# Unused columns in the first SBUF pools, so that matmul operands start at multiples of 256 bytes

## The chip, the cores and the metric

One core of a Trainium2 chip runs the whole kernel. The metric is the device time of one execution in microseconds (us). The median of three runs of the kernel before is 2657.34 us (2654.69 to 2658.03). SBUF is the on-chip memory with 128 partitions; every tile takes the same byte range in each partition, and its start in that range is what the change moves. PSUM holds the sums that TensorE (PE) writes. VectorE (DVE), ScalarE (ACT), GpSimd (POOL) and the sync engine (SP) work beside it.

## The reference

The kernel computes a trunk of two layers on 1024 frames of width 1024. Layer 0 mixes frames by banded softmax attention, layer 1 by a gated delta rule; each is followed by a dense squared-ReLU MLP of width 4096:

```
for i in range(DEPTH):
    if i % N_MIXERS == 0:
        x = x + chunked_rel_attention(rmsnorm(x, ...), w_qkv, rel_bias, w_o)
    else:
        x = x + gated_deltanet(rmsnorm(x, ...), w_in, conv_w, ..., w_o)
    x = x + squared_relu_mlp(rmsnorm(x, mlp_norm[i]), mlp_w_up[i], mlp_w_down[i])
return rmsnorm(x, final_norm)

def squared_relu_mlp(h, w_up, w_down):
    return jnp.square(jax.nn.relu(h @ w_up)) @ w_down
```

## The kernel before, in words

Each dense product is made of three matmuls on rounded halves: an operand x is split into `hi` (x rounded to the type fp32r) and `lo` (x - hi), and hi·hi, hi·lo and lo·hi are summed in one PSUM bank (`products`, L267, for q, k, v and the projections; `block_product`, L994, for the MLPs). A matmul streams its moving operand (`xhi`, `xlo`: 512 columns of 4 bytes, 2048 bytes in each partition) past a stationary operand of 128 columns (`whi`, `wlo`, `ahi`, `alo`, `a`: 512 bytes).

The MLPs multiply 2x2 blocks in the seven-product form of Strassen and Winograd. One of the 16 units of the up stage (`up`, L1073) is seven calls of `block_product` with four k steps, so 12 matmuls each, in this order: s1·t1, s2·t2, 12·21, s3·t3, s4·22, 22·t4, and 11·11 of the next unit. The blocks 11, 12, s4 and 22 of the weights lie in `whi` and `wlo`; the sums s1, s2 and s3 lie in `ahi` and `alo`. One of the 32 units of the down stage (`down`, L1309) is seven blocks of six matmuls in nearly the same order; after each block DVE adds the bank to the residual (L1365). In the down stage the right-hand operands lie in pool hp for the even steps of b and, but for "11", in pool hx for the odd ones (`rows_part`, L1226).

Tiles come from pools that are stacked in SBUF in the order in which they are opened. `Trunk.__init__` (L207) opens const, wp, hp, sm and np, which stay. Each stage then opens its own: pp and pb in attention; xa, xb and hx in an MLP; dq, d1 and db in the DeltaNet layer. A tile's start follows from the sizes of all that lies below it. The order of the instructions of each engine is recorded by the Python code (a planner with a modelled clock in attention and DeltaNet, a written order in the MLPs); no size of a tile enters it.

Of the kernel before, what the change touches and what calls it, by code (L numbers as in the profile page):

```python
# [7 lines left out]
F32 = mybir.dt.float32  # L8
# [8 lines left out]
P = 128  # L17
# [3 lines left out]
HB = 512  # L21
# [22 lines left out]
class Paced:  # L44


    def __init__(self, gens, slots):
        self.gens, self.slots = list(gens), slots
        self.total, self.done, self.at, self.n = sum(n for _, n in gens), 0, 0, len(gens)
# [156 lines left out]
class Trunk:  # L206
    def __init__(self, ctx, tc, a, phases=5):  # L207
        self.tc, self.nc, self.a = tc, tc.nc, a
        nc = self.nc
        self.const = ctx.enter_context(tc.tile_pool(name="const", bufs=1))  # L210
        self.wp = ctx.enter_context(tc.tile_pool(name="wp", bufs=2))
        self.hp = ctx.enter_context(tc.tile_pool(name="hp", bufs=1))
        self.sm = ctx.enter_context(tc.tile_pool(name="sm", bufs=2))
        self.dr = ctx.enter_context(tc.tile_pool(name="dr", bufs=1, space=DRAM))
        self.np = ctx.enter_context(tc.tile_pool(name="np", bufs=1))
        self.acc = ctx.enter_context(tc.tile_pool(name="acc", bufs=2, space=PSUM))
        self.n = 0
        self.wq = nc.sync
        self.ident = self.const.tile([P, P], F32, name="ident")
        make_identity(nc, self.ident)  # L220
        self.ones = self.const.tile([P, 1], F32, name="ones")
        nc.vector.memset(self.ones, 1.0)
        self.norms = self.const.tile([P, 5, KT], F32, name="norms")
        nc.scalar.dma_start(self.norms, a["norms"])

    def nm(self, s):
        self.n += 1
        return f"{s}_{self.n}"
# [1276 lines left out]
    def deltanet(self, rhs, finish):  # L1505

        tc = self.tc
        with ExitStack() as es:
            self.tpp = es.enter_context(tc.tile_pool(name="tp", bufs=2, space=PSUM))
            self.sc = es.enter_context(tc.tile_pool(name="sc", bufs=2, space=PSUM))  # L1510

            self.dq = es.enter_context(tc.tile_pool(name="dq", bufs=1))
            self.d1 = es.enter_context(tc.tile_pool(name="d1", bufs=1))
            self.db = es.enter_context(tc.tile_pool(name="db", bufs=2))
            self.drhs, self.finish = rhs, finish
            self.aux = lambda: self.tpp.tile([P, HB], F32, name=self.nm("tp"), tag="tp")
            rings = {
                "tp": Ring(2, self.aux), "acc": Ring(2, self.bank), "nt": Ring(3, self.nt),
                "s1": Ring(2, lambda: self.sc.tile([P, P], F32, name=self.nm("s1"), tag="s1")),
                "s2": Ring(2, lambda: self.sc.tile([P, P], F32, name=self.nm("s2"), tag="s2"))}  # L1520
            for t, n in (("xp", 2), ("cy", 2), ("cz", 2)):
                rings[t] = Ring(n, lambda t=t, n=n: self.db.tile([P, 4 + HB], F32, name=self.nm(t), tag=t, bufs=n))
            self.begin(rings)
            self.silu_at, self.ready_at, self.solved = 0.0, set(), {}
            return self.timed(self.dn_run)
# [180 lines left out]
    def dn_gates(self):  # L1706
        nc, a, rhs = self.nc, self.a, self.drhs
        d1, db = self.d1, self.db
# [8 lines left out]
        self.kd = self.dr.tile([8, P, S], F32, name="kd")  # L1717
        self.ud = self.dr.tile([2, P, 32, 32], F32, name="ud")
        self.u12 = self.dr.tile([8, 2, 32, 8, 32], F32, name="u12")
        self.Zh = []  # L1720
        for n in range(2):
            z = d1.tile([P, 8, P], F32, name=f"Zh{n}")
# [22 lines left out]
        av, bv = t64("av"), t64("bv")  # L1745
        nc.sync.dma_start(av, abd[0:8].rearrange("h (p t) -> (h p) t", t=P))
        nc.sync.dma_start(bv, abd[8:16].rearrange("h (p t) -> (h p) t", t=P))
        nea = d1.tile([NQ, 1], F32, name="nea")
        mask = d1.tile([P, P], F32, name="mask")
        nc.gpsimd.memset(mask, 0.0)  # L1750
# [746 lines left out]
```

## Time and profile before

| | us |
|---|---|
| median of three runs | 2657.34 |
| the profiled execution's own time | 2660.0 |
| its span, first to last instruction | 2657.9 |
| PE busy | 2514.9 (95%) |
| DVE busy | 1890.5 (71%) |
| POOL busy | 1305.2 (49%) |
| ACT busy | 1225.5 (46%) |

The span falls into six stages: attention (to about 555 us), the first MLP (up to about 905, down to about 1217), DeltaNet (to about 1876), a short projection, and the second MLP (up from about 1985, down from about 2310). Matmuls are pipelined, and the end of one is modelled in the trace, so that durations overlap; what one costs in a stream is read from the distance between starts.

### The profile page before, as it was taken

The page shows a single profiled execution, that of the slowest core. Times are in us where ns is not written, and L with a number is a line of the kernel's source. Part 1 is how long each engine was busy: PE and PEld are TensorE (multiplying, and loading weights), DVE is VectorE, ACT ScalarE, POOL GpSimd, SP SyncE. Part 2 cuts the span into 40 slices and gives each one's busy share as a digit, 9 for nine tenths or more (in the row PEclk, how much of TensorE's full clock was granted, in tenths as well). Part 3 has the DMA queues.
Part 4 walks back from the last instruction along what each step waited for, and adds up shares of the span by engine and source line. Part 5 has one row for each costly group of instructions (what it writes and reads, how often), then busy time and mean ns, then how long its engine had stood idle before and what let it go on. Part 6 is the DMA issues. An engine that isn't in the chain of part 4 may idle for free.

```text
span 2657.9 us, 36117 instructions
## 1 busy us (share of the span) xinstructions
PE 2514.9 (95%) x12638; PEld 2062.5 (78%) x12638; DVE 1890.5 (71%) x3287; ACT 1225.5 (46%) x2269; POOL 1305.2 (49%) x1100
## 2 busy tenths in 40 slices
PE   8999999989999999998888999999989999999997
PEld 6888888868888777776677788888777888777775
DVE  6665656675454899987579977666675445799997
ACT  6665667444344444434663343433343434444443
POOL 2443456242322688886464333333042232688886
PEclk9999999999999999999998999999999999999998
DMA  4222225224233423323453122213323323432322
GB/s 158 66 70 71 67 83 167 99 87 144 102 114 108 151 99 104 107 88 107 117 142 102 53 75 66 72 62 115 108 87 136 118 97 117 152 102 96 107 91 80
DMA packets 141814, 271.78 MB, mean 102 GB/s; under 512 B 49264, under 2 KB 55856, under 8 KB 141632
## 3 DMA queue, kind: packets, MB, share of 16 engines
q1 hardware_dynamic: 120752, 227.51, 27.3%
q10 hardware_dynamic: 20880, 41.97, 4.2%
q8 instruction: 99, 1.62, 0.3%
q14 instruction: 83, 0.68, 0.1%
HBM read 193.24 MB, written 67.80 MB: 98 GB/s over the span
## 4 chain that ended last, share of the span: by engine, by line
PE 73%; DVE 15%; issue 5%; DMA 2%; ACT 2%; POOL 2%; SPq 0%; DVEq 0%; ACTq 0%; POOLq 0%
PE y L1000 22%; PE acc L161 17%; PE z L1000 10%; PE acc L1000 6%; PE tp L161 3%; PE s L161 3%; PE po L161 2%; PE pt L161 2%; PE sp L161 2%; DVE x L1365 2%; PE acc L272 2%; PE acc L271 2%; PE acc L273 2%; DVE a L1006 2%; DVE ft L161 1%
## 5 line engine op out<-in xcount | busy, mean ns | idle before, releaser
L161 PE MATMUL acc<-xhi,whi 128*128 128x512 f32 (+1 forms) x904 | 372.5, 412 | 9.4 <-DVE xp L161 9.4
L1015 POOL TENSOR_TENSOR s<-wraw 128x256 f32<-128x256 f32 (+1 forms) x93 | 101.0, 1086 | 556.0 <-DMA wraw<-in_w_up_dram 396.6
L161 PE MATMUL acc<-xlo,whi 128*128 128x512 f32 (+1 forms) x904 | 372.0, 412 | 0.7 <-DVE xlo L387 0.7
L161 PE MATMUL acc<-xhi,wlo 128*128 128x512 f32 x896 | 367.4, 410 | 3.4 <-POOL wlo L161 3.4
L161 POOL TENSOR_TENSOR wlo<-wraw,whi 128x512 fp32r<-128x512 f32 x126 | 167.9, 1333 | 244.8 <-ACT whi L161 196.5
L1009 ACT ACTIVATE xhi<-r 128x512 fp32r<-128x512 f32 x224 | 135.9, 628 | 256.5 <-POOL r L1012 207.2
L1006 DVE TENSOR_TENSOR wlo<-wraw,whi 128x512 fp32r<-128x512 f32 (+1 forms) x184 | 200.8, 1092 | 50.7 <-ACT whi L1009 47.4
L1000 PE MATMUL y<-xhi,whi 128*128 128x512 f32 x504 | 202.2, 401 | 14.8 <-DVE ssum L1083 8.7
L1000 PE MATMUL y<-xhi,wlo 128*128 128x512 f32 x504 | 201.8, 400 | 13.6 <-DVE wlo L1006 13.6
L1012 POOL TENSOR_TENSOR r<-r,r 128x512 f32<-128x512 f32 x124 | 202.9, 1638 | 14.8 <-DVE xlo L1006 10.2
L1000 PE MATMUL y<-xhi,a 128*128 128x512 f32 x488 | 180.2, 410 | 23.6 <-DVE x L1365 23.0
L1000 PE MATMUL y<-xlo,whi 128*128 128x512 f32 x504 | 200.7, 398 | 0.0
L161 PEld LDWEIGHTS acc<-xhi,whi 128*128 128x128 f32 (+1 forms) x904 | 171.9, 190 | 34.2 <-DVE xp L161 6.9
L161 PEld LDWEIGHTS acc<-xhi,wlo 128*128 128x128 f32 x896 | 171.0, 191 | 28.9 <-POOL wlo L161 4.7
L161 PEld LDWEIGHTS acc<-xlo,whi 128*128 128x128 f32 (+1 forms) x904 | 172.1, 190 | 24.9 <-DVE xlo L387 1.2
L1365 DVE TENSOR_TENSOR x<-y,x 128x512 f32<-128x512 f32 x240 | 163.8, 683 | 13.7 <-PE y L1000 11.8
L1009 ACT ACTIVATE whi<-wraw 128x512 fp32r<-128x512 f32 (+2 forms) x191 | 143.7, 766 | 37.5 <-ACT g L1086 12.7
L1083 DVE TENSOR_TENSOR ssum<-acc,nt 128x512 f32<-128x512 f32 x32 | 22.1, 691 | 189.1 <-PE acc L1000 189.1
L161 POOL TENSOR_SCALAR pr<-pr,rs 128x640 f32<-128x640 f32 (+4 forms) x128 | 88.6, 696 | 129.5 <-DVE rs L161 96.8
L1000 PEld LDWEIGHTS y<-xhi,a 128*128 128x128 f32 x488 | 92.6, 190 | 66.9 <-DVE x L1365 45.0
L161 POOL TENSOR_TENSOR cy<-cy,cz 128x512 f32<-128x512 f32 x48 | 69.1, 1439 | 145.6 <-DVE cz L161 131.5
L1004 POOL TENSOR_TENSOR xlo<-r,xhi 128x512 fp32r<-128x512 f32 x84 | 109.1, 1299 | 41.6 <-ACT xhi L1009 40.9
(349 smaller groups left out, 7131.1 us busy)
## 6 DMA issues: line engine op xcount, KB each, us to landing
wraw<-in_w_up_dram SPq DMA_DIRECT2D x64, 512.0 KB, 3.4
wraw<-in_w_down_dram SPq DMA_DIRECT2D x64, 512.0 KB, 3.9
r<-gd SPq DMA_DIRECT2D x112, 256.0 KB, 2.7
gd<-ssum ACTq DMA_DIRECT2D x64, 256.0 KB, 2.0
gd<-g ACTq DMA_DIRECT2D x64, 256.0 KB, 2.3
wraw<-in_w_in_dram SPq DMA_DIRECT2D x32, 512.0 KB, 3.5
wraw<-in_w_qkv_dram SPq DMA_DIRECT2D x30, 512.0 KB, 3.4
x<-xd SPq DMA_DIRECT2D x24, 512.0 KB, 5.0
```

What stands on the lines that cost most here:

```text
L161: return call(*args, **more)
L271: nc.tensor.matmul(ps, hi[:, k], xh, start=(k == 0), stop=False)
L272: nc.tensor.matmul(ps, hi[:, k], xl, start=False, stop=False)
L273: nc.tensor.matmul(ps, lo[:, k], xh, start=False, stop=(k == KT - 1))
L1000: nc.tensor.matmul(ps, w[:, k], x, start=bool(first and f), stop=bool(last and e), skip_group_check=True)
L1004: self.nc.gpsimd.tensor_tensor(lo, src, hi.bitcast(F32), ALU.subtract)
L1006: self.nc.vector.tensor_tensor(lo, src, hi.bitcast(F32), ALU.subtract)
L1009: self.nc.scalar.activation(hi, src, AF.Copy)
L1012: self.nc.gpsimd.tensor_tensor(out, x, y, ALU.subtract)
L1015: self.nc.gpsimd.tensor_tensor(out, x, y, ALU.add)
L1083: nc.vector.tensor_tensor(g, c, t, ALU.add)
L1365: nc.vector.tensor_tensor(x, ps, x, ALU.add)
```

## The change: what it does

Five tiles that nothing reads or writes are put into pools, and the three ring tiles of the convolution grow from 4 + 512 to 64 + 512 columns. Of these tiles the same columns are used as before.

```diff
@@ Trunk.__init__
+        self.const.tile([P, 32], F32, name="room0", tag="room0")
         self.ident = self.const.tile([P, P], F32, name="ident")
...
         nc.scalar.dma_start(self.norms, a["norms"])
+        self.const.tile([P, 16], F32, name="room1", tag="room1")
+        self.sm.tile([P, 24], F32, name="room2", tag="room2", bufs=1)
@@ deltanet
-                rings[t] = Ring(n, lambda t=t, n=n: self.db.tile([P, 4 + HB], F32, name=self.nm(t), tag=t, bufs=n))
+                rings[t] = Ring(n, lambda t=t, n=n: self.db.tile([P, 64 + HB], F32, name=self.nm(t), tag=t, bufs=n))
@@ dn_gates
         self.u12 = self.dr.tile([8, 2, 32, 8, 32], F32, name="u12")
+        d1.tile([P, 16], F32, name="room3")
         self.Zh = []
...
         nc.sync.dma_start(bv, abd[8:16].rearrange("h (p t) -> (h p) t", t=P))
+        d1.tile([P, 40], F32, name="room4")
         nea = d1.tile([NQ, 1], F32, name="nea")
```

The built programs have the same instructions in the same order on every engine, with the same waits; only the addresses of SBUF operands differ. Where the operands start, as the remainder of the byte address by 256:

| tiles | pool | before | after |
|---|---|---|---|
| ident (of the transposes) | const | 128 | 0 |
| whi, wlo, wraw (weights) | wp | 64 | 0 |
| xhi, xlo of the normed input, and half of the MLP's right-hand operands | hp | 64 | 0 |
| ssum, R, nt | np | 224 | 0 |
| q, khi, klo, V, pr, thi, tlo (attention) | pp, pb | 224 | 0 |
| ahi, alo, a, the other right-hand operands xhi and xlo, residual x (MLP) | xa, xb, hx | 224 | 0 |
| kn, qT, vT, kbg (DeltaNet) | dq | 224 | 0 |
| Zh, vn, qk (DeltaNet) | d1 | 160 | 0 |
| kd, WQ, vb, st (DeltaNet) | db | 192 | 0 |

Before, 64, 128 and 192 are multiples of 64 and 160 and 224 are not. Of the fp32r matmuls of 512 columns, 4832 have both operands at 64, 1758 the moving one at 224 and the stationary one at 64, 1728 the other way round, and 554 both at 224. What is at 64 lies in the first 92,000 bytes of a partition, and the matmul operands at 224 lie above that.

## Rows read from the trace of the kernel before

**Rows 1.** The page: the span, and the chain's shares by engine.

```profile
span 2657.9 us, 36117 instructions
...
PE 73%; DVE 15%; issue 5%; DMA 2%; ACT 2%; POOL 2%; SPq 0%; DVEq 0%; ACTq 0%; POOLq 0%
```

**Rows 2.** Busy time by window: attention, up, down, DeltaNet; us, busy and count.

```profile
200.00:400.00 200.00, 200.00 (x1172) 173.84 (x1171) 121.08 (x321) 124.97 (x274) 90.10 (x98) 1.00 0.27 74
...
720.00:900.00 180.00, 175.75 (x752) 140.73 (x751) 98.65 (x119) 77.26 (x121) 61.69 (x47) 1.00 0.34 116
900.00:1100.00 200.00, 191.35 (x810) 150.21 (x810) 186.29 (x254) 83.59 (x147) 172.33 (x142) 1.00 0.33 110
...
1600.00:1800.00 200.00, 195.95 (x1379) 172.09 (x1379) 138.72 (x351) 79.49 (x172) 66.31 (x49) 1.00 0.22 69
```

**Rows 3.** Timeline of PE, an up unit: each block's first matmul; start, us.

```profile
739.71 0.40 PE L1000 MATMUL z<-xhi,ahi 128*128 128x512 f32 x1
...
742.52 0.39 PE L1000 MATMUL y<-xhi,ahi 128*128 128x512 f32 x1
...
745.32 0.40 PE L1000 MATMUL acc<-xhi,whi 128*128 128x512 f32 x1
...
748.13 0.40 PE L1000 MATMUL y<-xhi,ahi 128*128 128x512 f32 x1
...
750.93 0.39 PE L1000 MATMUL z<-xhi,whi 128*128 128x512 f32 x1
...
753.73 0.39 PE L1000 MATMUL y<-xhi,whi 128*128 128x512 f32 x1
...
756.47 0.40 PE L1000 MATMUL y<-xhi,whi 128*128 128x512 f32 x1
...
759.27 0.40 PE L1000 MATMUL z<-xhi,ahi 128*128 128x512 f32 x1
```

**Rows 4.** Timeline of PE, a down unit with even b: blocks' first matmuls.

```profile
1000.57 0.39 PE L1000 MATMUL z<-xhi,whi 128*128 128x512 f32 x1
...
1001.93 0.39 PE L1000 MATMUL y<-xhi,whi 128*128 128x512 f32 x1
...
1004.66 0.39 PE L1000 MATMUL z<-xhi,a 128*128 128x512 f32 x1
...
1006.06 0.41 PE L1000 MATMUL y<-xhi,a 128*128 128x512 f32 x1
...
1007.49 0.39 PE L1000 MATMUL acc<-xhi,whi 128*128 128x512 f32 x1
...
1008.88 0.39 PE L1000 MATMUL y<-xhi,a 128*128 128x512 f32 x1
```

**Rows 5.** Waits from 900 to 1100 us: total us, times, longest.

```profile
PEld y L1000 <- DVE x L1365: 16.2, 21, 2.3
...
PE y L1000 <- DVE x L1365: 8.6, 11, 1.9
```

**Rows 6.** Timeline of PE in attention.

```profile
302.06 0.39 PE L161 MATMUL acc<-xhi,whi 128*128 128x512 f32 x1
302.29 0.40 PE L161 MATMUL acc<-xlo,whi 128*128 128x512 f32 x1
...
303.92 0.31 PE L161 MATMUL sp<-khi,q 128*128 128x320 f32 x1
304.07 0.31 PE L161 MATMUL sp<-klo,q 128*128 128x320 f32 x1
...
304.51 0.40 PE L161 MATMUL acc<-xhi,whi 128*128 128x512 f32 x1
304.75 0.49 PE L161 MATMUL pt<-ident,pr 128*128 128x128 f32 x3
```

**Rows 7.** ACT groups by form: busy us, mean ns, idle before.

```profile
L1009 ACT ACTIVATE whi<-wraw 128x512 fp32r<-128x512 f32 x126 | 76.1, 625 | 23.8 <-PE y L1000 8.8 <-PE acc L1000 6.3 <-POOL wraw L1012 4.9
...
L1009 ACT ACTIVATE ahi<-s 128x512 fp32r<-128x512 f32 x96 | 60.6, 632 | 38.0 <-ACT ssum L1086 22.6 <-PE y L1000 9.6 <-ACT g L1086 4.0
```

## The prediction

> **What bounds the kernel now.** The page's head and its chain of waits come first: in the chain that ends last, PE has 73% and DVE 15%, waits for DMA 2% [rows 1]. Then the busy time by window, stage by stage. In the up stage PE is busy for 175.75 us of 180, and of DVE, ACT and POOL none for more than 98.65; in attention PE fills all 200 us of its window; in the down stage PE has 191.35 of 200, and DVE is close behind with 186.29 [rows 2]. So in most of the time the pace is set by how fast PE takes one matmul after another, and in the down stage by PE and DVE in turns.
>
> The change adds no instruction, no wait and no byte that is moved; it moves addresses alone. It can pay only if the duration of an instruction depends on where its operands start. Whether it does can be looked up in the trace of before, because operands of both kinds stand there side by side. That is the third view, the timeline of PE, read by the starts of the blocks.
>
> In one up unit all seven blocks have 12 matmuls of 512 columns [rows 3]. The first five have one operand at remainder 64 and the other at 224: s1·t1 from 739.71 to 742.52, 2.81 us; s2·t2, 12·21 and s3·t3 2.80, 2.81 and 2.80; s4·22 from 750.93 to 753.73, 2.80. The sixth, 22·t4, has both operands at 64: 753.73 to 756.47, 2.74 us. The seventh, 11·11, again has one of each: 756.47 to 759.27, 2.80. Per matmul that is 233 to 234 ns against 228. The same engine, the same shape, no idle time before either, the same stage: the slower blocks are those in which an operand starts off a multiple of 64.
>
> The down stage repeats it [rows 4]: the block s4·22, six matmuls with both operands at 64, takes from 1000.57 to 1001.93, 1.36 us or 227 ns each; 22·t4 and 11·11 after it, both operands at 64, together 2.73 for twelve; s1·t1 and s2·t2, with the stationary one at 224, take 1.40 (1004.66 to 1006.06) and 1.43 (1006.06 to 1007.49). The block 12·21, both at 64 but between two others, takes 1.39.
>
> **The change part by part.**
>
> *The up stages.* After the change every block has both operands at a multiple of 64, so I price each like the one that has that already, 2.74 us. A mixed block falls from 2.81 or 2.80 to that: six of them take 14.02 + 2.80 = 16.82 us now [the starts in rows 3: 14.02 from 739.71 to 753.73, 2.80 from 756.47 to 759.27], and would take 6 x 2.74 = 16.44. That is 0.38 us of a unit of 19.56 us. There are 16 units in each of two layers: 32 x 0.38 = 12.2 us. Nothing else is near the bound there (98.65 us of DVE in 180), so this arrives whole. Bounds: if a stream of blocks with no change of operand kind is as fast as 1.36 us for six [rows 4], a block is 2.72 and a unit saves 19.56 - 19.04 = 0.52, so 16.6 us in all; if the weight sums' producers (DVE and ACT) come later than the matmuls that want them, half, 6.1.
>
> *The down stages.* In a unit with an even b the blocks s1·t1, s2·t2 and s3·t3 are mixed; in an odd one both operands of these, or the moving one of 12·21, s4·22 and 22·t4, are at 224, so six blocks of seven are touched. The nearest price is 1.40 against 1.37 (half of 2.73), 0.03 us a block. Per layer that is 16 x 0.09 + 16 x 0.18 = 4.3 us, 8.6 for both. Here the cover is thin: in 200 us, PE and its weight loads wait 8.6 and 16.2 us for DVE's addition at L1365 [rows 5]. What PE gains ahead of such a wait is lost in it. I take half, 4.3 us; the bounds are 0 and 8.6.
>
> *Attention.* The dense products have both operands at 64 already: 302.06 to 302.29, 0.23 us. The short matmuls read q, khi, klo, V, thi and tlo, all at 224: 0.15 us for 320 columns (303.92 to 304.07), and a dense matmul ahead of others takes 0.24 (304.51 to 304.75) [rows 6]. There are 960 of the short ones, and no row shows one at a multiple of 64. If each lost what a 512-column one loses in rows 3, (2.80 - 2.74)/12 = 5 ns, that is 4.8 us; if the loss goes with the number of columns, about half as much. The planner's order is fixed, and a wait of another engine may take some back. I take 3.0 us, between 0 and 4.8.
>
> *DeltaNet.* Its dense products are at 64 already, and its scan alternates between PE and DVE in matmuls of 128 columns; PE is busy for 195.95 us of 200 [rows 2], but with many matmuls that are not fp32r. No row separates them by address. I take 0, with 2 us on either side.
>
> *The other engines.* ACT's rounding takes 625 ns from and to tiles at 64 and 632 ns at 224 [rows 7]: 7 ns in 630, on an engine that is under half busy, so 0. The wider convolution tiles hold the same columns, and no instruction on them grows. The DMAs move the same bytes; their 2% of the chain [rows 1], some 53 us, bounds what addresses could do for them, and if a tenth of that went either way it would be 5 us. I take 0.
>
> Sum: 12.2 + 4.3 + 3.0 = 19.5 us. The profiled execution took 2660.0 us (its span of 2657.9 [rows 1] and 2.1 around it), so 2640.5 is what such an execution should take; the median of the runs is 2.7 us lower than it, 2657.34, and I predict 2637.8, rounded to 2638.
>
> **The rivals.**
>
> *Nothing happens, because it isn't the remainder.* All operands at 64 lie low in SBUF and those at 224 lie above them, so the slow blocks could be slow for their region. The change shifts everything by some hundred bytes and leaves the regions as they are: 2657. Against it: in rows 4 the two sums s1·t1 and s2·t2 read the same pools and differ by 0.03 us, so that the region alone doesn't set the time; for it: no row has a high tile at a multiple of 64 in a 512-column matmul.
> The Trainium skill bears on this rival: SBUF — State Buffer, Specifications (TRN2), says that SBUF is read in lines of 16 bytes and that only crossing into a new line costs. All remainders before (64, 128, 160, 192, 224) are multiples of 16, so by that rule the change would be worth nothing, and the time 2657. The trace doesn't agree with it as the only rule, since 2.80 and 2.74 us stand next to each other in rows 3. Its section Operand start alignment states the legal starts and says of its own measurements that they timed nothing.
>
> *More than that: only a multiple of 256 is free.* Then the blocks at 64 pay as well, and the step from 224 to 64 shows only a part. If the step from 64 to 0 is worth as much again, 5 ns, on each of the 8872 matmuls of 512 columns (4832 + 1758 + 1728 + 554), 44 us come on top: about 2594. For it speaks nothing in the rows, as none has remainder 0 there; against it, that the two kinds at 64 and 224 differ at all although both are off 256.
>
> *PE gains and the others take it back.* If DVE's additions set the pace of the whole down stage and the planned stages wait elsewhere, only half of the up stages' 12.2 us remains: 6.1 us, 2651. Rows 5 speak for it in the down stage; the up stage, where DVE has 98.65 us of 180, speaks against it.
>
> *Slower: streams that start at the same remainder collide.* While one matmul streams, the weights of the next are loaded. With both at the same remainder, the two reads may meet more often; 12·21 in rows 4, both at 64, took 1.39 us and not 1.36, and s2·t2 took 1.43. If every block became as slow as the 1.43, an up block would take 2.86 and a unit 20.02 instead of 19.56: 32 x 0.46 = 14.7 us more, and down units 7 x 1.43 = 10.01 instead of some 9.7, half of it felt, 64 x 0.15 = 9.6 us: 2682. It decides if the mean block of 12 is above 2.80 us. Against it: the two blocks whose operands share the remainder 64 in rows 3 and 4 are the fastest of all.
>
> **How the numbers follow.** My forecast has a chance of 0.72; the time of no change 0.09; the larger gain 0.07; the gain taken back 0.07; the slower case 0.05. The range of the forecast itself: with all upper bounds, 16.6 + 8.6 + 4.8 + 2 + 5 = 37.0 us, 2620; with all lower ones, the up stages' 6.1 alone, 2651. 2620 to 2652 holds that case and the gain taken back, and leaves out the three others, 0.21; since part of the larger gain would fall within it, this is about 8 in 10. Within 0.2%, 5.3 us, a measurement of this kernel can't be told from no change, so faster means under 2652. Faster: 0.72 + 0.07 and most of the 0.07 taken back, 0.84. Same: 0.09 and the rest, 0.11. Slower: 0.05.
>
> **What would show it.** Right: in the up stage of the changed kernel the starts of the blocks lie 2.72 to 2.75 us apart throughout, and units 19.05 to 19.2 us instead of 19.56; in the down stage s1·t1 and s2·t2 take 1.36 to 1.38, while DVE's waits for banks fall and PE's waits at L1365 grow; ACT's and POOL's means stay. Wrong: blocks that still differ by the pool they read (the region), blocks well under 2.70 (only 256 is free), blocks over 2.80 (the collision), or units of 19.1 us with a span that hasn't moved (a wait that took it back, to be looked for at L1365 and in the planned stages).

## The result, and the profile after

The changed kernel takes 2641.61 us (median of 4 runs, 2639.70 to 2646.91), the kernel before 2656.91 beside it (2654.69 to 2658.03): a ratio of 0.9947, 95% interval 0.9929 to 0.9964. The gain is 15.3 us; 19 were forecast, and the range held the time. The two profiled executions lie further apart than the medians (2660.0 and 2639.7 us), so what is read from this pair of traces adds up to 20 us and not to 15.

The page after, span and chain by engine [rows 1]:

```profile
span 2637.9 us, 36117 instructions
...
PE 70%; DVE 18%; issue 6%; ACT 3%; DMA 2%; POOL 1%; SPq 0%; ACTq 0%; DVEq 0%; POOLq 0%
```

PE's share of the chain falls from 73% to 70%, and DVE's rises from 15% to 18%. Busy time by window, in the columns of [rows 2] (PE, PEld, DVE, ACT, POOL, each with its count, then clock, DMA share, GB/s):

```profile
200.00:400.00 200.00, 200.00 (x1173) 174.24 (x1172) 121.40 (x322) 125.29 (x275) 90.24 (x98) 1.00 0.25 73
720.00:900.00 180.00, 174.09 (x759) 142.81 (x758) 103.34 (x127) 79.01 (x125) 65.33 (x49) 0.99 0.36 126
900.00:1100.00 200.00, 191.79 (x817) 151.41 (x817) 185.18 (x252) 82.54 (x146) 176.13 (x145) 1.00 0.31 103
1600.00:1800.00 200.00, 195.97 (x1380) 172.10 (x1379) 139.15 (x350) 79.55 (x172) 67.14 (x50) 1.00 0.23 74
```

The timeline of PE in an up unit after, first matmul of each block [rows 3]:

```profile
736.98 0.39 PE L1004 MATMUL z<-xhi,ahi 128*128 128x512 f32 x1
...
739.70 0.39 PE L1004 MATMUL y<-xhi,ahi 128*128 128x512 f32 x1
...
742.42 0.39 PE L1004 MATMUL acc<-xhi,whi 128*128 128x512 f32 x1
...
745.14 0.39 PE L1004 MATMUL y<-xhi,ahi 128*128 128x512 f32 x1
...
747.86 0.39 PE L1004 MATMUL z<-xhi,whi 128*128 128x512 f32 x1
...
750.58 0.39 PE L1004 MATMUL y<-xhi,whi 128*128 128x512 f32 x1
...
753.30 0.39 PE L1004 MATMUL y<-xhi,whi 128*128 128x512 f32 x1
...
756.02 0.39 PE L1004 MATMUL z<-xhi,ahi 128*128 128x512 f32 x1
```

Every block takes 2.72 us, 226.7 ns per matmul, and the unit 19.04 us instead of 19.56: the upper bound of the forecast's term, not its middle. 22·t4 and 11·11, 2.74 and 2.80 before, take 2.72 each as well (750.58, 753.30, 756.02).

The same view in a down unit with even b [rows 4]:

```profile
993.81 0.40 PE L1004 MATMUL z<-xhi,whi 128*128 128x512 f32 x1
...
995.19 0.39 PE L1004 MATMUL y<-xhi,whi 128*128 128x512 f32 x1
...
997.91 0.39 PE L1004 MATMUL z<-xhi,a 128*128 128x512 f32 x1
...
999.55 0.50 PE L1004 MATMUL y<-xhi,a 128*128 128x512 f32 x1
...
1001.04 0.39 PE L1004 MATMUL acc<-xhi,whi 128*128 128x512 f32 x1
...
1002.41 0.39 PE L1004 MATMUL y<-xhi,a 128*128 128x512 f32 x1
```

12·21 now takes 1.37 us (1001.04 to 1002.41) instead of 1.39, but from s1·t1 to s2·t2 it takes 1.64 (997.91 to 999.55), and s2·t2 itself 1.49. The forecast had 1.36 to 1.38 for these two; there is a stall in each. The waits from 900 to 1100 us (total us, times, longest) [rows 5]:

```profile
PEld y L1004 <- DVE x L1369: 17.7, 25, 1.3
...
POOL xlo L1008 <- ACT xhi L1013: 14.9, 20, 0.7
...
PE y L1004 <- DVE x L1369: 7.5, 10, 0.8
```

PE and its weight loads wait 25.2 us for the addition in this window, before it was 24.8: the growth that the forecast named doesn't show here. DVE's waits for PE's banks, which were to fall, rose (for z from 8.4 to 10.7 us).

In attention the short matmuls still take 0.15 us for 320 columns [rows 6], as the timeline of PE after shows:

```profile
303.26 0.31 PE L161 MATMUL sp<-khi,q 128*128 128x320 f32 x1
303.41 0.30 PE L161 MATMUL sp<-klo,q 128*128 128x320 f32 x1
```

Of ACT's groups by form, whi keeps its 625 ns and ahi its 632 [rows 7], although both now read and write multiples of 256; so the 7 ns between them don't come from these remainders:

```profile
L1013 ACT ACTIVATE whi<-wraw 128x512 fp32r<-128x512 f32 x126 | 76.1, 625 | 21.4 <-PE acc L1004 6.1 <-POOL wraw L1016 4.8 <-PE y L1004 3.2
...
L1013 ACT ACTIVATE ahi<-s 128x512 fp32r<-128x512 f32 x96 | 60.6, 632 | 38.2 <-ACT ssum L1090 22.2 <-ACT g L1090 7.2 <-PE y L1004 6.4
```

Where the time went, by PE's progress: the two traces have the same instructions on PE, so the stage that ends with a given matmul can be subtracted. The same for four other runs against the profile of before (us; the run names are explained below):

| stage | forecast | after | e_all32 | e_nodelta | e_room2 | e_sm32 |
|---|---|---|---|---|---|---|
| attention | -3.0 | -1.2 | -2.1 | -1.1 | -0.6 | -0.2 |
| two up stages | -12.2 | -14.3 | -15.1 | -15.0 | -14.6 | -0.8 |
| two down stages | -4.3 | -1.3 | -3.2 | -0.9 | -0.9 | -2.9 |
| DeltaNet and projection | 0 | -3.1 | -0.4 | -0.1 | +3.4 | +3.1 |

The last line differs in sign between runs whose DeltaNet operands all start alike: it scatters by 3 us from execution to execution, and 3 us of the 20 between the profiles of before and after are of this kind. The down stages scatter as much: the -1.3 after are +1.8 in the first and -3.1 in the second, and e_sm32 has 0.0 and -2.9.

### The profile page after: what moved, and what is told of

Same layout as the page of the kernel before. It is cut to its first block, busy times and chain, and to the rows that moved or that the text cites. A ratio compares the mean times of both kernels' runs of the same rounds, so it can differ in the third digit from the quotient of the medians.

```text
span 2637.9 us, 36117 instructions
## 1 busy us (share of the span) xinstructions
PE 2492.1 (94%) x12638; PEld 2061.5 (78%) x12638; DVE 1886.2 (72%) x3287; ACT 1225.0 (46%) x2269; POOL 1310.9 (50%) x1100
## 4 chain that ended last, share of the span: by engine, by line
PE 70%; DVE 18%; issue 6%; ACT 3%; DMA 2%; POOL 1%; SPq 0%; ACTq 0%; DVEq 0%; POOLq 0%
PE y L1004 20%; PE acc L161 17%; PE z L1004 9%; PE acc L1004 6%; PE tp L161 3%; DVE x L1369 3%; DVE a L1010 3%; PE s L161 3%; PE po L161 2%; PE pt L161 2%; PE sp L161 2%; PE acc L276 2%; PE acc L277 2%; PE acc L275 2%; DVE ft L161 2%
## 5 line engine op out<-in xcount | busy, mean ns | idle before, releaser
L1016 POOL TENSOR_TENSOR r<-r,r 128x512 f32<-128x512 f32 x124 | 204.1, 1648 | 13.6 <-DVE xlo L1010 13.3
L1369 DVE TENSOR_TENSOR x<-y,x 128x512 f32<-128x512 f32 x240 | 163.6, 682 | 8.9 <-PE y L1004 8.5
L1010 DVE TENSOR_TENSOR a<-s,a 128x256 fp32r<-128x256 f32 x117 | 129.7, 1109 | 0.0
```

Source lines behind the costliest of these rows:

```text
L1010: self.nc.vector.tensor_tensor(lo, src, hi.bitcast(F32), ALU.subtract)
L1016: self.nc.gpsimd.tensor_tensor(out, x, y, ALU.subtract)
L1369: nc.vector.tensor_tensor(x, ps, x, ALU.add)
```

## The experiments

**Which addresses count, on matmuls alone.** A kernel of matmuls on zeros, in blocks of 24 of one kind; `mv` is moving, `st` stationary, and with the letters a to g an operand starts at remainder 0, 4, 16, 32, 48, 64 or 128:

```diff
+            for k in range(n):
+                nc.tensor.matmul(bank[:, :cols], st[w][:, k % 3, ow : ow + P], mv[m][:, k // 3 % 3, om : om + cols], ...)
```

> Nothing but matmuls on tiles of zeros (no part of the trunk is computed): blocks of 24 fp32r matmuls with other weights each time, no other engine beside them. The moving operand starts 0, 4, 16, 32, 48, 64 or 128 bytes after a multiple of 256 (tiles mva to mvg), the stationary one likewise (sta to stg). Theory A (an operand off a multiple of 64 bytes costs, each by itself): 0, 64 and 128 take the same, about 227 ns a matmul of 512 columns, and 4, 16, 32 and 48 cost 4 to 7 ns more, for either operand. Theory B (only unlike remainders cost): blocks with both operands at the same remainder take 227 ns whatever it is, unlike ones 233. Theory C (only 256 is free): 64 and 128 cost like 32. Theory D (lines of 16 bytes): 16, 32 and 48 take the same as 0, only 4 costs. For 384, 320, 256 and 128 columns: theory A 4 to 5 ns more at 32 whatever the length, or less in proportion; the after run says about 0.

One run. Mean distance of starts, with a pair written as (moving, stationary): (0,0) 226.7 ns; with the moving one at 4, 16, 32, 48, 64, 128 and the stationary one at 0: 236.5, 231.8, 232.7, 233.1, 229.3, 232.3; the other way round 232.3, 233.3, 233.4, 233.3, 233.2, 232.2. So 64 and 128 are not free against 0, which speaks against the theory of the prediction. With both at 32, 64 or 128 the mean is 227.5, 228.6 and 228.5, because the first ones, up to about ten, still vary and the rest repeat 226, 227, 227. But both at 4, 16 and 48 give 237.5, 231.3 and 230.1, and (32,16) and (32,48) are as fast as 226.7, while (16,32) and (48,32) take 235.0 and 231.4: at remainders that aren't multiples of 32, likeness is not the rule. Shorter matmuls show nothing: 384 columns 173.3 to 174.5, 320 columns 146.3 to 146.9, 256 columns 118.0 to 119.7 for the four pairs of 0 and 32.

**The kernel before, what lies above sm at a multiple of 256 (but for parts of DeltaNet) and the weights left at 64.**

```diff
+        self.sm.tile([P, 8], F32, name="room2", tag="room2", bufs=1)
```

> The kernel before with one unused tile of 8 columns (32 bytes) in the pool sm and nothing else: np and all later pools move from remainder 224 to 0, while const, wp and hp stay at 64 (and the DeltaNet tiles of db move from 192 to 224). Theory A: all 512-column operands at multiples of 64, so the whole gain: up units of 19.07 to 19.1 us, median 2638 to 2645, ratio 0.993 to 0.996. Theory C or remainders that have to be the same modulo 256: mixed blocks keep 2.80 us, units 19.5, median 2655 to 2659.

Measured: 2661.13 us, ratio 1.0012 (1.0003 to 1.0021). Every operand of the 512-column matmuls is at a multiple of 64, and nothing is gained. The up unit in its timeline:

```profile
740.78 0.40 PE L1001 MATMUL z<-xhi,ahi 128*128 128x512 f32 x1
...
743.58 0.40 PE L1001 MATMUL y<-xhi,ahi 128*128 128x512 f32 x1
...
746.38 0.39 PE L1001 MATMUL acc<-xhi,whi 128*128 128x512 f32 x1
...
749.18 0.40 PE L1001 MATMUL y<-xhi,ahi 128*128 128x512 f32 x1
...
751.94 0.39 PE L1001 MATMUL z<-xhi,whi 128*128 128x512 f32 x1
```

The first three blocks take 2.80 us as before the change, and so do s4·22 and 11·11; s3·t3 takes 2.76 (749.18 to 751.94). Here the theory that a multiple of 64 suffices fell.

**The changed kernel, everything 32 bytes further.**

```diff
-        self.const.tile([P, 32], F32, name="room0", tag="room0")
+        self.const.tile([P, 40], F32, name="room0", tag="room0")
```

> The changed kernel with its first unused tile 8 columns wider: every operand of the matmuls lies at 32 instead of 0, all alike. Theory A: every 512-column block pays, the dense ones in attention and DeltaNet too: 8872 x 4 ns = 35 us over the changed kernel, where PE sets the pace, so 2665 to 2680, up units 19.5 to 19.7. Theory B: remainders are alike, so as the changed kernel, 2638 to 2645, up units 19.1.

Measured: 2641.81 us, ratio 0.9940 (0.9928 to 0.9952): the whole gain, with every operand of these matmuls at 32 and none at a multiple of 64.

```profile
733.93 0.39 PE L1004 MATMUL z<-xhi,ahi 128*128 128x512 f32 x1
...
736.65 0.39 PE L1004 MATMUL y<-xhi,ahi 128*128 128x512 f32 x1
...
739.37 0.39 PE L1004 MATMUL acc<-xhi,whi 128*128 128x512 f32 x1
```

**The changed kernel without the DeltaNet part** (no room3 and room4, the ring tiles as before):

```diff
-        d1.tile([P, 16], F32, name="room3")
-        d1.tile([P, 40], F32, name="room4")
-                rings[t] = ... [P, 64 + HB] ...
+                rings[t] = ... [P, 4 + HB] ...
```

> The changed kernel without its DeltaNet part (no room3, no room4, convolution tiles of 4 + 512 columns again), so that Zh, vn, qk, kd, WQ, vb and st lie off 256 again and the rest at 0. If their remainders don't matter (128-column fp32 matmuls): as the changed kernel, 2638 to 2645. If they were worth the 3 us by which the DeltaNet stage was shorter after the change: 2643 to 2648, and the stretch of that stage as long as before.

Measured: 2642.93 us, ratio 0.9943 (0.9931 to 0.9956). That part of the change is worth nothing that can be measured.

**Matmuls alone, second series,** one run: blocks of 36, moving at 0 (a) or 32 (d), stationary at 0, 32, 64 and so on to 256 (a, d, e to k), then pairs in turn, then fewer columns.

```diff
+                    block([m + w], HB)
+            block(["aa", "dd"], HB, 72)
+            block(["ad", "da"], HB, 72)
+            for cols in (504, 480, 448, 416):
```

> Matmuls on zeros alone, in blocks of 36; none of the reference is computed. Moving operand at remainder 0 or 32, stationary at 0, 32, 64 ... 224 and 256. Theory B (likeness of the two remainders, period 256): (0,0), (32,32) and (0,256) settle at 226.7 ns from start to start, all others stay at 229 to 235. If the period were shorter than 256 (64 or 128), (0,64) or (0,128) would settle at 226.7 too in blocks that are longer than those of the first series. A rival on the mechanism: a stream collides with the load of the NEXT weights, so that likeness to the next matmul's stationary operand counts and not to its own. Alternating pairs tell: (0,0),(32,32) in turn have own alike and next unlike, (0,32),(32,0) in turn own unlike and next alike. Theory B as I put it (own pair): the first 226.7, the second 231 to 235; the rival: the reverse. At 504, 480, 448 and 416 columns I look for the width from which an unlike pair costs: at 512 it costs 5 to 8 ns, at 384 nothing was seen, so the cost should be gone somewhere between.

The timeline of PE, where one line is a block of 36:

```profile
22.27 8.33 PE L43 MATMUL pv<-mva,sta 128*128 128x512 f32 x36
30.43 8.55 PE L43 MATMUL pw<-mva,std 128*128 128x512 f32 x36
38.82 8.56 PE L43 MATMUL px<-mva,ste 128*128 128x512 f32 x36
...
89.05 8.32 PE L43 MATMUL pv<-mva,stk 128*128 128x512 f32 x36
97.20 8.57 PE L43 MATMUL pw<-mvd,sta 128*128 128x512 f32 x36
105.61 8.36 PE L43 MATMUL px<-mvd,std 128*128 128x512 f32 x36
113.81 8.55 PE L43 MATMUL pu<-mvd,ste 128*128 128x512 f32 x36
122.20 8.56 PE L43 MATMUL pv<-mvd,stf 128*128 128x512 f32 x36
```

From one line's start to the next: (0,0) 8.16 us for 36, (0,32) 8.39, (0,64) 8.41; (0,256) 8.15; (32,0) 8.41, (32,32) 8.20, (32,64) 8.39. The stationary remainder minus the moving one, by 256, gives the same mean whether the moving one is at 0 or 32: for 0, 32, 64, 96, 128, 160, 192, 224 it is 226.7, 233.2, 233.4, 234.0, 232.5, 233.1, 228.8, 233.3 ns (227.6 for (32,32), which starts unsettled). So the period is 256, and for these two moving remainders only the difference counts; (64,0) and (128,0) of the first series, 229.3 and 232.3, fit in at 192 and 128. But a difference doesn't always have one price: in e_sm32 the pairs of s1·t1, s2·t2 and s3·t3 are all (64,0), and the first two take 2.80 us for 12, 233 ns each, where s3·t3 comes down to 229 in its second half. What decides between the two, no run shows.

The pairs in turn: own pair alike and the next weights unlike: 232.0 ns in the mean. Own pair unlike and the next weights alike: 230.0, and after the first every distance is 230. Neither the theory (226.7 for the first) nor the rival (226.7 for the second) holds: a matmul's own pair does not decide alone, and of the orders tried only a run of matmuls that are all alike has the whole gain. At 504 columns the alike pair still takes 226.7, (0,32) 229.9 and (32,0) 227.1; at 480, 216.8, 216.6 and 220.0; at 448, 202.6, 204.4 and 206.3; at 416, 188.4, 190.0 and 193.3. So at 416 columns an unlike pair still costs 2 to 5 ns; at 384, in the first series, it costs nothing.

**The kernel before with one line**, room2 of 24 columns, which puts np and what lies above it, but for parts of DeltaNet (d1 and db), at 64 like the weights:

```diff
+        self.sm.tile([P, 24], F32, name="room2", tag="room2", bufs=1)
```

> The kernel before with one line of the change, the unused 24 columns in pool sm: np and all pools above it start at remainder 64 and not 224, as wp and hp do. Nothing is at a multiple of 256. Theory B (only likeness counts): the whole gain, 2638 to 2645 us, ratio about 0.994, blocks of 12 in the up stage 2.72 us. Theory C (only a multiple of 256 is free): no change, 2657. The theory of the prediction (a multiple of 64 suffices) expects the same as B; it was the other run with room in sm, where mixed remainders 0 and 64 stayed slow, that spoke against it.

Measured: 2643.43 us, ratio 0.9946 (0.9934 to 0.9959), blocks of 2.72 us. One unused tile does it, and against e_sm32 only its width differs.

**Why the down stages gain so little: less work for DVE.** In both layouts, in `rows`:

```diff
-                self.low(l, src, h, name in PLO)
+                if name in PLO:
+                    self.low(l, src, h, True)
+                else:
+                    self.high(l, src)
```

> The kernel before, except that in the down stage those lower halves of the right-hand operands which DVE makes are replaced by a rounding copy on ACT (other values, as much PE work, less DVE work). It is the baseline for the next run, and should itself be some 10 to 25 us faster than the kernel before, since waits for DVE in the down stages fall: 2632 to 2647.

> The changed kernel with the same edit: lower halves that DVE makes in the down stage become a rounding copy on ACT. If the gain of the down stages was lost to DVE's additions, it now stays: the distance between this and the run with the layout of before grows from about 15 to 20 us to 21 to 26 us, and each down stage is 3 to 4 us shorter than with the layout of before, where it was not shorter at all between before and after. If the down stages gain nothing for another reason (their streams of 6 matmuls are too short to settle), the distance stays at 15 to 20 us and the down stages stay level.

Measured: 2625.92 and 2604.65 us, a distance of 21.3 (against the kernel before 0.9878, 0.9863 to 0.9893, and 0.9797, 0.9784 to 0.9811). The distance grew as expected, but the down stages keep only part: -1.3 and -2.7 us, where 3 to 4 each were expected. Of the others, -3.6 stands in DeltaNet, which scatters. The first of the two runs is faster than its expected range: 32 us, of which 17.2 and 18.2 stand in the down stages. DVE's subtractions a<-s,a of 512 columns fall there from 1151 to 682 ns, and POOL's differences from 1603 to 1464 (900 to 1100 us), though nothing in either was changed, as DVE's groups show:

```profile
L1006 DVE TENSOR_TENSOR a<-s,a 128x512 fp32r<-128x512 f32 x20 | 13.6, 682 | 0.0
```

POOL's groups in the same run and window:

```profile
L1012 POOL TENSOR_TENSOR r<-r,r 128x512 f32<-128x512 f32 x41 | 60.0, 1464 | 2.3 <-ACT xlo L1009 2.3
```

**Half of DVE's addition.**

```diff
-                nc.vector.tensor_tensor(x, ps, x, ALU.add)
+                nc.vector.tensor_tensor(x[:, :256], ps[:, :256], x[:, :256], ALU.add)
```

> The kernel before, except that in the down stages DVE's addition of a block to the residual (L1365) covers 256 of the 512 columns, so the other half of the sums is left out. DVE's part falls from about 683 to 350 ns. Baseline for the next run. If DVE's addition is what PE waits for, it should be 20 to 45 us faster than the kernel before.

> The changed kernel with the same half addition. In the profiles of before and after, the streams of the down stages gain 231.3 to 227.8 ns per matmul, some 4.3 us a stage, and the waits for DVE's addition grow by as much (distances over 245 ns: 33.9 to 46.7 us in the first, 35.3 to 39.4 in the second). Theory: the addition paces the down stages. Then with half of it away the gain stays, 3.5 to 5 us a stage, and the distance from the run with the layout of before is 22 to 27 us. Rival: another order of the down stage (ACT's rounding, POOL's sums, the next weights) takes it back whatever DVE does; then the distance stays at 15 to 20 us and the distances over 245 ns grow again in the layout of after.

Measured: 2655.19 and 2640.20 us, distance 15.0; the first is 0.9991 of the kernel before (0.9982 to 1.0000). The additions fell to 416 ns and next to nothing came of it: the down stages differ by 0.0 and +0.4 us. The theory on record fell. POOL's groups in the second run, that with the changed layout, 900 to 1100 us (busy, mean ns, idle before and its releaser), show what is full instead:

```profile
L1016 POOL TENSOR_TENSOR r<-r,r 128x512 f32<-128x512 f32 x39 | 65.2, 1673 | 0.0
L1008 POOL TENSOR_TENSOR xlo<-r,xhi 128x512 fp32r<-128x512 f32 x30 | 43.0, 1433 | 14.8 <-ACT xhi L1013 14.8
L1019 POOL TENSOR_TENSOR s<-wraw 128x256 f32<-128x256 f32 x19 | 22.1, 1165 | 0.6 <-DVE a L1010 0.6
L1016 POOL TENSOR_TENSOR s<-s,wraw 128x256 f32<-128x256 f32 x19 | 20.3, 1069 | 1.5
```

POOL is busy for 182.28 us of these 200 and idle for about 18 more, of which 14.8 are ACT's rounding of what POOL has just made; it never waits for PE.

**Half of POOL's differences.** In both layouts:

```diff
-            self.psub(r11, r12, r11)
+            self.psub(r11[:, :256], r12[:, :256], r11[:, :256])
```

and so for the three others.

> The kernel before, except that in the down stages POOL's four differences of the right-hand operands (psub in `rows`, shown as r<-r,r) cover 256 of 512 columns; the other half of these operands is left as it was loaded. That takes some 30 us of POOL's 172 in 200. Baseline for the next run. If POOL paces the down stages, both are shorter, and the whole 20 to 40 us faster than the kernel before; if DVE's length does, it is nearly as slow as before.

> The changed kernel with the same half differences on POOL. In the two runs with half of DVE's addition the distance between the layouts stayed at 15.0 us, and POOL's busy time and its waits for ACT's rounding filled the window of 200 us. Theory: POOL's chain (difference, ACT's rounding, low half) paces the down stages, and PE's waits for DVE's addition are what it looks like from PE. Then with POOL relieved the gain of the down stages stays, 3 to 5 us a stage, and the distance from the run with the layout of before is 21 to 26 us. Rival: DVE with its full additions paces them as well; then the distance stays at 14 to 20 us and the distances over 245 ns between matmuls grow again in the layout of after.

Measured: 2636.08 and 2609.83 us, a distance of 26.3 (0.9916, 0.9898 to 0.9933, and 0.9820, 0.9805 to 0.9834, of the kernel before). By progress the down stages differ by -4.0 and -6.9 us (one pair of profiles, with the scatter of 3 us a stage), together no less than the 8.6 that the prediction had before it halved them. The window 900 to 1100, first the layout of before:

```profile
900.00:1100.00 200.00, 198.09 (x843) 156.19 (x842) 188.95 (x265) 88.31 (x154) 157.54 (x149) 1.00 0.35 115
```

and then that of after:

```profile
900.00:1100.00 200.00, 199.85 (x867) 161.89 (x867) 181.74 (x267) 88.42 (x154) 161.03 (x154) 1.00 0.32 109
```

PE is now full, at 867 matmuls against 843, where the change alone made 817 out of 810 [rows 2]. With POOL's work relieved the faster streams arrive. POOL alone doesn't pace the down stages, though: half of its differences shortens them by 11.4 and 13.3 us in the layout of before, and less of DVE's subtractions by 17.2 and 18.2. So both kinds of work set the pace, and the length of the addition doesn't; why the gain of the layout stays whole with the one relieved (-4.0 and -6.9) and in part with the other (-1.3 and -2.7) is open.

## Why the prediction was right, and where it wasn't

**The number held, the mechanism did not.** The step that failed: "the slower blocks are those in which an operand starts off a multiple of 64". Each slow block of [rows 3] had such an operand, but each was also a pair of unlike remainders, 64 and 224, and the only fast one was a pair of equal ones. e_sm32 parts the two: all at multiples of 64, the same blocks unlike, no gain. e_all32 does from the other side: all at 32, the whole gain. The price per block was read from a pair that was alike, and the change makes all pairs alike, so the forecast came out all the same. That was luck: the same reasoning gives the whole gain for e_sm32, which has none. The trace of before could have shown it: its 431 matmuls in the down stages with both operands at 224 and another such behind them stand 230.6 ns apart in the mean, those with both at 64 229.0, and the unlike ones 233.7 and 234.0. I hadn't read these.

The Trainium skill, SBUF — State Buffer, Who interferes with whom, gives PE two read ports, one for the moving operand and one for the weight load, that are independent of each other, and says that PE never waits for anyone. By that an operand's start against the other's would be worth nothing; m_micro2 measures 226.7 against 228.8 to 234.0 ns, so here the measurement decides. Which part of the chip makes the difference no run shows.

**The up stages: the sum held, its size was low.** 12.2 us forecast, 14.3 in the profile after and 14.6 to 15.1 in three other runs. The term used 2.74 us for an alike block that stood between unlike ones and so had not settled; in an unbroken row it is 2.72, which was the upper bound. The 16.6 us of that bound weren't reached: a steady unit saves the 0.5 us, but the first and the last unit of a stage less, and some of the early ones have a stall of 0.2 to 0.6 us in them.

**The down stages: half wasn't enough.** The streams gained what was forecast: the mean of all distances up to 245 ns fell from 231.4 to 227.8 ns in the first down stage (up to about 1205 us), some 4.4 us, and the longer distances grew from 33.9 to 46.7 us in sum. Part of that growth is only that more distances are longer than 245 ns, 107 instead of 77 in the whole stage; what they hold beyond 245 ns grew by 5.8 us, so that the gain was lost. The count of blocks in the sum was wrong by the rule found: of the six that it touched in a unit with odd b, the three with both operands at 224 were alike already. They, and the blocks with both at 64, still gained some 2 ns a matmul as their neighbours became alike, and so the sum came out near. PE's wait for DVE at L1369, which I named, is real, but it is the last link only. e_halfadd shows that it doesn't hang on the length of the addition, e_halfpool that it hangs on POOL's differences, and e_lessdve that it hangs on DVE's subtractions too. In the timeline of DVE after, the addition always takes 0.68 us, and it stands behind subtractions that don't:

```profile
1022.62 0.68 DVE L1010 TENSOR_TENSOR xlo<-r,xhi 128x512 fp32r<-128x512 f32 x1
...
1026.70 1.58 DVE L1010 TENSOR_TENSOR a<-s,a 128x512 fp32r<-128x512 f32 x1
1028.21 0.68 DVE L1369 TENSOR_TENSOR x<-y,x 128x512 f32<-128x512 f32 x1
...
1040.96 0.67 DVE L1010 TENSOR_TENSOR wlo<-wraw,whi 128x512 fp32r<-128x512 f32 x1
```

The timeline of POOL beside it:

```profile
1022.63 1.82 POOL L1016 TENSOR_TENSOR r<-r,r 128x512 f32<-128x512 f32 x1
...
1026.45 1.28 POOL L1016 TENSOR_TENSOR r<-r,r 128x512 f32<-128x512 f32 x1
```

DVE's subtraction of 512 columns takes 0.67 or up to 1.58 us, and POOL's 1.28 or 1.82: as if one of the two were held up while both run. In these lines it is the one that starts later: POOL's 1.82 starts at 1022.63, just behind DVE's 0.68, and DVE's 1.58 at 1026.70, behind POOL's 1.28. The Trainium skill, SBUF — State Buffer, Who interferes with whom, says that a DVE instruction with two SBUF inputs contends with a GpSimd instruction that reads SBUF, and one with at most one doesn't. The trace agrees: the addition reads one operand from PSUM and stays at 0.68. e_lessdve fits it, where fewer of DVE's subtractions made POOL's differences shorter. e_halfpool and e_lessdve each take away work and this contention at once; which of the two counts more is open.

**Attention: 3.0 forecast, 1.2 measured** (0.6 to 2.1 in the other runs with like remainders). Scatter is nearly as large: e_halfadd_before, in the layout of before, is 0.9 us shorter there. The 5 ns of a 512-column matmul don't exist for the short ones: at 320 columns m_micro has 146.3 to 146.9 ns for the four pairs of 0 and 32. And khi, klo, q and the other operands at 224 were alike before.

**DeltaNet, ACT, DMA: 0, and it stands** (e_nodelta), within the scatter of 3 us.

**The rivals.** "It isn't the remainder" fell with the blocks of 2.72 us; "only a multiple of 256 is free" with e_all32; "the others take it back" came true for the down stages alone. "Streams that start at the same remainder collide" is the reverse of what was found. Still open is what lies behind the rule: (16,16) is slow, (32,16) is fast, pairs in turn lie between, and (64,0) has two prices.

## What to carry to other kernels

Where a stage is bound by rows of 512-column fp32r matmuls, let all moving and stationary operands start at one remainder by 256, a multiple of 32: unlike pairs cost 2 to 7 ns of 227 each, and one unused tile of 24 columns saved 14.5 us of 2658 here. Before one reads a cause from slow and fast groups of a trace, list in what else the groups differ, and look for the group that has the one and not the other. A wait names the engine that came last; whether that engine sets the pace is told by making its work shorter.

## What was unexpected on the chip

- A stream of 512-column fp32r matmuls runs in a fixed pattern of distances: 226, 227, 227 ns for alike operands, 235, 232, 235, 232, 235, 231 for (0,32). After a change of kind the alike pair takes up to ten matmuls to get there: 236, 224, 231, 236, 228, 233, 231, and then 226, 227, 227, for (32,32) after (32,0).
- 504 columns of an alike pair take as long as 512, 226.7 ns.
- With DVE's additions of the down stages cut from 683 to 416 ns the kernel lost only 1.9 us of 2657: POOL's and DVE's other instructions there grew longer, r<-r,r on POOL from 1603 to 1704 ns and wlo<-wraw,whi on DVE from 899 to 1149.
